# A hybrid gMLP and retention encoder on one core: retention scores of the first 128 keys from float32r halves, one tile later

## The chip, the core and the metric

The kernel runs on one core of a Trainium2 chip. The metric is device time in microseconds (us) for one execution. Times of whole executions are medians of several runs; everything about single instructions comes from one profiled execution.

Names of engines in the profile: PE is the matrix engine, PEld its weight loads, DVE the vector engine, ACT the scalar engine, POOL the engine that here mostly issues transfers, SP the queue that streams the weights in.

## The reference, cut to what matters

A two-layer encoder step on 256 prompt frames and 32 sample frames (288 columns in all). Layer 0 mixes tokens with a gated MLP, layer 1 with retention; each is followed by a SwiGLU network. All in float32. The change lies in the retention block of layer 1, which has 8 heads:

```python
def retention_block(q, k, v, s0, decay, inner, zeta, blk_decay):
    scores = jnp.einsum('bhqd,bhkd->bhqk', q, k) * decay[None]
    intra = jnp.einsum('bhqk,bhkv->bhqv', scores, v)
    cross = jnp.einsum('bhqd,bhdv->bhqv', q, s0) * inner[None, :, :, None]
    s_new = blk_decay[None, :, None, None] * s0 + jnp.einsum(
        'bhkd,bhkv->bhdv', k * zeta[None, :, :, None], v)
    return intra + cross, s_new
```

A head has 256 dimensions for q and k (rotated by `rope` first) and 512 for v. The output of a head is normalised, gated by `silu(g)` and multiplied by `w_out`.

## The kernel before, in words

**Weights.** All weights lie in one stream in the order of use, cut into chunks of 8 blocks of 128x128. SP loads a chunk as float32 (`raw`). ACT makes its high half `whi` in float32r, the reduced form that PE takes in one pass (`split`, L454), and DVE the low half `wlo`, the rest (L455). There are four buffers of each half; `prep(c + 3)` stands where PE begins chunk c, so a chunk is made while three others lie ahead of it.

**The main products.** Activations are held as halves too, transposed (features on partitions, 288 columns). One block is three matmuls of 288 columns: high by high (L106), low by high (L107), high by low (L108). A tile is one output tile of 128 features: 16 blocks, 48 matmuls, two chunks. `core.tick()` runs after each tile, and `core.after(n, f)` puts off a piece of work by n tiles. PE executes in the order in which the program is written. DVE, ACT and POOL have an order of their own, which a scheduler made from the dependencies and from costs it assumes; each of them works through its list strictly in that order.

**Retention.** `b_in` gives a head 4 tiles of v, 2 of k, 2 of q and 4 of g. Heads 0 and 1 take g, v, k, q in this order; the others v, k, q, and g of heads 2 and 3 comes behind q of head 3, of 6 and 7 behind q of head 7. Heads 2, 3 and 7 follow the q of the head before without g between. What happens around the change:

- `turn` (at once after the second k or q tile, two tiles later for head 0) rotates k or q on DVE with `rope` (L668 to L673) into `rk` or `rq`. For k, ACT repeats the 32 sample columns twice (L717), so that the sample has 96 stationary columns; then DVE transposes k (L740) and POOL sends it through memory to turn it to rows (`k_room`, `kw`). For q, DVE and ACT make `qi`.
- `k_split` scales and splits the rows of k into `kh`, `kl`, `ks`.
- `scores` (`core.after(self.wait, ...)` behind q; `self.wait` is 3 for head 0 and 2 for the others) has six matmuls in float32: two of 128 keys by 256 prompt queries (L770), two of the second 128 keys by the second 128 queries (L772), two of 96 stationary columns by 32 sample queries (L774). Each float32 matmul shows up as two in the profile. DVE multiplies by the decay `dec` into `pf` and `psf` (L779 to L781); ACT and DVE split these into `ph`, `pl` and `r_ps` (L454, L455, L783, L784).
- `attend` stands one tile behind the last of `scores`, `k_split` and `v_split`: 28 float32r matmuls (`os`, `ss`, `ob`, `sp`), the first of which reads `r_ps`. The head's output is then normalised and moved through memory (`o_room`, `of`); `o_gate` multiplies it by the gate (L894) and splits it for `b_out`.
- v goes from DVE transposes (`tv`, L700) through memory (`v_room`, `vw`, `vz`, on POOL) to `v_split` three tiles later (ACT and DVE write `vv`).

Small buffers of the rotation and of the scores (`rt1`, `rt2`, `qf`, `pf`, `psf`) each have a place in the pool of the retention stage. `PostNorm.tmp` gives out six rotating buffers of another pool, used by the normalisations before and behind.

Of the kernel before, what the change touches and what calls it, by code (L numbers as in the profile page):

```python
# [10 lines left out]
F32 = mybir.dt.float32  # L11
F32R = mybir.dt.float32r
I32 = mybir.dt.int32
AF = mybir.ActivationFunctionType
ALU = mybir.AluOpType
# [4 lines left out]
P = 128  # L20
D = 2048
KT = D // P
NP = 256
NS = 32
NT = NP + NS
# [3 lines left out]
NR = 3 * NS  # L29
# [146 lines left out]
def fourth(nc):  # L176

    def mm(out, w, x, **kw):
        nc.tensor.matmul(turned(out, 4), w, turned(x, 4), **kw)

    return mm
# [271 lines left out]
def split(nc, hi, lo, f):  # L453
    nc.scalar.copy(hi, f)  # L454
    nc.vector.tensor_tensor(lo, f, hi.bitcast(F32), ALU.subtract)  # L455
# [176 lines left out]
def retention(core, cst, x, y, lnp, prev, ins, st_p_out, st_s_out):  # L632
    tc, nc = core.tc, core.nc
    xh, xl = x
    xs = lambda k: (xh[:, k, :NT], xl[:, k, :NT])
    mm, mm4 = nc.tensor.matmul, fourth(nc)
    with ExitStack() as es:
        pool = es.enter_context(tc.tile_pool(name="ret", bufs=1, reuse_waits="tile"))
# [10 lines left out]
        nc.gpsimd.dma_start(inn, ins["inner"])  # L649
        ln = PostNorm(core, cst, x, y, lnp, 2)  # L650
        pss = pool.tile([P, 2 * NS], F32R, tag="pss", name="r_ps")
        zero = pool.tile([P, NS], F32, name="r_zero")
        nc.gpsimd.memset(zero, 0.0)
        nc.scalar.copy(pss[:NR, NS:], zero[:NR, :])
        heads = {}
# [7 lines left out]
            return t[:, :4 * NT].rearrange("p (b i s) -> p b i s", b=9, i=4)  # L663

        def rope(dst, a, b, cos, sin, nm):
            t1 = pool.tile([P, NT], F32, tag="rt1", name=f"rt1{nm}", bufs=1)
            t2 = pool.tile([P, NT], F32, tag="rt2", name=f"rt2{nm}", bufs=1)
            nc.vector.tensor_tensor(t1, a[:, :NT], cos, ALU.mult)  # L668
            nc.vector.tensor_tensor(t2, b[:, :NT], sin, ALU.mult)
            nc.vector.tensor_tensor(dst[:, 0, :NT], t1, t2, ALU.subtract)  # L670
            nc.vector.tensor_tensor(t1, a[:, :NT], sin, ALU.mult)
            nc.vector.tensor_tensor(t2, b[:, :NT], cos, ALU.mult)
            nc.vector.tensor_tensor(dst[:, 1, :NT], t1, t2, ALU.add)  # L673

        class Head:
            def __init__(self, h):
                self.h = h
                self.wait = 3 if h == 0 else 2
                self.ps = {}
                self.left = {"k", "v", "s"}  # L680
                self.open = {"o", "g"}
                self.dec = pool.tile([P, NT], F32, tag="dec", name=f"dec{h}")
                nc.gpsimd.dma_start(self.dec, ins["decay"][h])
                self.sg = pool.tile([P, 4, NT], F32, tag="rsg", name=f"rsg{h}", bufs=2)

            def evac(self, m, ps):
                h = self.h
                if m < 32:
                    self.ps[m % 2] = ps
                    if m % 2:  # L690
                        turn = lambda p=dict(self.ps): self.turn(m, p)
                        if h == 0:
                            core.after(2, turn)
                        else:
                            turn()
                elif m < 64:
                    i = m % 4
                    if i == 0:
                        self.tv = blocks(f"tv{h}", h)
                    nc.vector.transpose(self.tv[:, :, i, :], ps[:, :NT])  # L700
                    if i == 3:
                        self.v_move()
                else:
                    i = m % 4
                    nc.scalar.activation(self.sg[:, i, :], ps[:, :NT], AF.Silu)
                    if i == 3:
                        core.after(1, lambda: self.o_gate("g"))

            def turn(self, m, ps):
                h = self.h  # L710
                isk = m >= 16
                nm = ("k" if isk else "q") + str(h)
                r = pool.tile([P, 2, NP + (NR if isk else NS)], F32, tag="kr" if isk else "qr", name="r" + nm)
                rope(r, ps[0], ps[1], cs[:, 0, :], cs[:, 1, :], nm)
                if isk:
                    self.kr = r
                    nc.scalar.copy(r[:, :, NT:].rearrange("p d (r n) -> p d r n", r=2),  # L717
                                   r[:, :, NP:NT].unsqueeze(2).broadcast_to([P, 2, 2, NS]))
                    self.k_move()
                else:  # L720
                    self.qr = r
                    qf = pool.tile([P, 2, NS], F32, tag="qf", name=f"qf{h}")
                    qi = pool.tile([P, 160], F32R, tag="qi", name=f"qi{h}")
                    self.qi = qi[:, 20:20 + 4 * NS].rearrange("p (d a n) -> p d a n", d=2, a=2)
                    nc.vector.tensor_tensor(qf, r[:, :, NP:], inn[:, h, :].unsqueeze(1).broadcast_to([P, 2, NS]), ALU.mult)
                    split(nc, self.qi[:, :, 0, :], self.qi[:, :, 1, :], qf)
                    core.after(self.wait, self.scores)

            def proceed(self, what, i=3):
# [35 lines left out]
            def scores(self):  # L765
                h = self.h
                self.proceed("s")
                b = core.bank(f"sc{h}")
                for d in range(2):
                    mm(b[:, 0:NP], self.kr[:, d, 0:P], self.qr[:, d, 0:NP], start=d == 0, stop=d == 1)  # L770
                for d in range(2):
                    mm(b[:, NP:NP + P], self.kr[:, d, P:NP], self.qr[:, d, P:NP], start=d == 0, stop=d == 1)  # L772
                for d in range(2):
                    mm(b[:NR, 384:384 + NS], self.kr[:, d, NP:], self.qr[:, d, NP:], start=d == 0, stop=d == 1)  # L774
                pf = pool.tile([P, 384], F32, tag="pf", name=f"pf{h}")
                self.ph = pool.tile([P, 384], F32R, tag="ph", name=f"ph{h}")
                self.pl = pool.tile([P, 384], F32R, tag="pl", name=f"pl{h}")
                psf = pool.tile([P, NS], F32, tag="psf", name=f"psf{h}")
                nc.vector.tensor_tensor(pf[:, :NP], b[:, :NP], self.dec[:, :NP], ALU.mult)  # L779
                nc.vector.tensor_tensor(pf[:, NP:], b[:, NP:384], self.dec[:, :P], ALU.mult)  # L780
                nc.vector.tensor_tensor(psf[:NR, :], b[:NR, 384:384 + NS], self.dec[:NR, NP:], ALU.mult)  # L781
                r = slice(2 * NS, NR)
                nc.scalar.copy(pss[:NR, :NS], psf[:NR, :])  # L783
                nc.vector.tensor_tensor(pss[r, :NS], psf[r, :], pss[r, :NS].bitcast(F32), ALU.subtract)  # L784
                split(nc, self.ph, self.pl, pf)

            def v_move(self):
                h = self.h
# [135 lines left out]
        for grp in range(2):  # L924
            a, b, c, d = order[4 * grp:4 * grp + 4]
# [12 lines left out]
def hybrid_step(ctx, tc, ins, outs):  # L938
# [34 lines left out]
    ln = gmlp(core, cst, x, y, lnp, ins, outs["v"], lambda s: load(s + 4))  # L973
    ln = ffn(core, cst, x, y, lnp, 0, ln)
    ln = retention(core, cst, x, y, lnp, ln, ins, outs["st_p"], outs["st_s"])
    ffn(core, cst, x, y, lnp, 1, ln, outs["yT"])
    core.flush()
# [86 lines left out]
```

## Time and profile before

| | |
|---|---|
| median of 3 runs | 2777.39 us (2776.27 to 2778.74) |
| the profiled execution | 2780.03 us, its span 2778.3 us |
| PE busy | 2767.8 us |
| DVE, ACT, POOL busy | 1664.5, 1241.0, 140.9 us |
| PE's weight loads busy | 2753.8 us |
| scores, attend of head 2 on PE | from 1330.86 us, from 1338.63 us |

The span goes from the first to the last instruction; the execution has 1.7 us more around it. Matmul records overlap, since the matmuls are pipelined, so what a matmul costs is read from the distance between the starts of neighbours, or from the chain of waits, where each piece is given the time up to the next. Times of single instructions are counted from the start of the span.

### The profile page before, as it was taken

The numbers are of one execution on the slowest core, as the hardware profiler recorded it, in microseconds if no ns is written. First come the engines' busy times: TensorE is split into PE (matmuls) and PEld (weight loads), VectorE is DVE, ScalarE is ACT, GpSimd is POOL, SyncE is SP. The second block draws the span as 40 slices with busy tenths as digits, with TensorE's granted clock in tenths as the row PEclk, the third lists the DMA queues.
The fourth block names the chain that finished last, engine by engine and source line by source line (L and its number), as shares of the span: only waits on it lengthen the run. The fifth ranks groups of instructions, "written<-read, shape, count | busy, mean of one in ns | idle before, by whom it ended". The sixth has DMA issues, their size and how long they took to land.

```text
span 2778.3 us, 51413 instructions
## 1 busy us (share of the span) xinstructions
PE 2767.8 (100%) x21590; PEld 2753.8 (99%) x21590; DVE 1664.5 (60%) x2360; ACT 1241.0 (45%) x1644; POOL 140.9 (5%) x241
## 2 busy tenths in 40 slices
PE   9999999999999999999999999999999999999998
PEld 9999999999999999999999999999999999999998
DVE  5688854444444466767765666767844455444465
ACT  5455643433333344644443444445634333343343
POOL 1100000000000000012200111200000000000001
PEclk9999999999999999999999999999999999999999
DMA  8655555555555555567765676765555555555553
GB/s 277 214 186 167 168 175 175 175 174 172 172 174 174 176 175 176 190 209 232 232 196 175 195 221 214 229 197 171 173 173 172 173 174 175 175 174 173 172 173 125
DMA packets 147529, 515.51 MB, mean 186 GB/s; under 512 B 18064, under 2 KB 22176, under 8 KB 147264
## 3 DMA queue, kind: packets, MB, share of 16 engines
q1 hardware_dynamic: 132928, 473.33, 52.0%
q0 software_dynamic: 14224, 38.59, 4.7%
q8 instruction: 169, 2.77, 0.4%
q14 instruction: 64, 0.52, 0.0%
q10 hardware_dynamic: 144, 0.29, 0.0%
HBM read 486.98 MB, written 25.17 MB: 184 GB/s over the span
## 4 chain that ended last, share of the span: by engine, by line
PE 97%; DMA 1%; DVE 1%; ACT 0%; issue 0%; POOL 0%; SPq 0%; DVEq 0%; POOLq 0%; ACTq 0%
PE af_in L107 13%; PE af_in L108 13%; PE af_in L106 13%; PE ab_in L106 7%; PE ab_in L107 7%; PE ab_in L108 7%; PE af_out L106 6%; PE af_out L107 6%; PE af_out L108 6%; PE ab_out L107 2%; PE ab_out L106 2%; PE ab_out L108 2%; PE aa_in L108 2%; PE aa_in L106 2%; PE aa_in L107 2%; PE aa_out L107 1%
## 5 line engine op out<-in xcount | busy, mean ns | idle before, releaser
L455 DVE TENSOR_TENSOR wlo<-raw,whi 128x1024 fp32r<-128x1024 f32 (+1 forms) x892 | 1086.2, 1219 | 885.5 <-ACT whi L454 881.4
L454 ACT CAST whi<-raw 128x1024 fp32r<-128x1024 f32 (+1 forms) x892 | 933.1, 1047 | 1384.5 <-issue 336.5
L107 PE MATMUL af_in<-xl,whi 128*128 128x288 f32 (+1 forms) x2816 | 812.6, 289 | 0.0
L106 PE MATMUL af_in<-xh,whi 128*128 128x288 f32 (+1 forms) x2816 | 812.3, 288 | 0.0
L108 PE MATMUL af_in<-xh,wlo 128*128 128x288 f32 (+1 forms) x2816 | 812.3, 288 | 0.0
L108 PEld LDWEIGHTS af_in<-xh,wlo 128*128 128x128 f32 x2816 | 527.7, 187 | 0.0
L107 PEld LDWEIGHTS af_in<-xl,whi 128*128 128x128 f32 x2816 | 527.7, 187 | 0.0
L106 PEld LDWEIGHTS af_in<-xh,whi 128*128 128x128 f32 x2816 | 527.7, 187 | 0.0
L106 PE MATMUL ab_in<-xh,whi 128*128 128x288 f32 (+1 forms) x1536 | 443.9, 289 | 0.0
L107 PE MATMUL ab_in<-xl,whi 128*128 128x288 f32 (+1 forms) x1536 | 443.3, 289 | 0.0
L108 PE MATMUL ab_in<-xh,wlo 128*128 128x288 f32 (+1 forms) x1536 | 443.2, 289 | 0.0
L108 PE MATMUL af_out<-hh,wlo 128*128 128x288 f32 x1408 | 405.9, 288 | 0.0
L106 PE MATMUL af_out<-hh,whi 128*128 128x288 f32 x1408 | 405.9, 288 | 0.0
L107 PE MATMUL af_out<-hl,whi 128*128 128x288 f32 x1408 | 405.9, 288 | 0.0
L107 PEld LDWEIGHTS ab_in<-xl,whi 128*128 128x128 f32 x1536 | 287.9, 187 | 0.3
L106 PEld LDWEIGHTS ab_in<-xh,whi 128*128 128x128 f32 x1536 | 287.9, 187 | 0.3
L108 PEld LDWEIGHTS ab_in<-xh,wlo 128*128 128x128 f32 x1536 | 287.9, 187 | 0.0
L107 PEld LDWEIGHTS af_out<-hl,whi 128*128 128x128 f32 x1408 | 263.8, 187 | 0.0
L106 PEld LDWEIGHTS af_out<-hh,whi 128*128 128x128 f32 x1408 | 263.8, 187 | 0.0
L108 PEld LDWEIGHTS af_out<-hh,wlo 128*128 128x128 f32 x1408 | 263.8, 187 | 0.0
L108 PE MATMUL aa_in<-xh,wlo 128*128 128x288 f32 x512 | 148.1, 289 | 1.2 <-DVE wlo L455 1.1
L106 PE MATMUL aa_in<-xh,whi 128*128 128x288 f32 x512 | 148.7, 290 | 0.0
(240 smaller groups left out, 2873.9 us busy)
## 6 DMA issues: line engine op xcount, KB each, us to landing
raw<-in_wpack_dram SPq DMA_DIRECT2D x887, 512.0 KB, 3.3
v_room<-tv POOLq DMA_DIRECT2D x32, 144.0 KB, 5.1
of<-o_room POOLq DMA_DIRECT2D x32, 144.0 KB, 5.2
vw<-v_room POOLq DMA_DIRECT2D x8, 512.0 KB, 5.2
out_st_s_dram<-sso POOLq DMA_DIRECT2D x16, 256.0 KB, 2.6
out_st_p_dram<-so POOLq DMA_DIRECT2D x16, 256.0 KB, 2.8
o_room<-to POOLq DMA_DIRECT2D x8, 512.0 KB, 3.8
y<-in_xT_dram SPq DMA_DIRECT2D x8, 288.0 KB, 5.2
```

The lines of the kernel that those rows point to most:

```text
L106: mm(ps, hi, xh, start=first, stop=False)
L107: mm(ps, hi, xl, start=False, stop=False)
L108: mm(ps, lo, xh, start=False, stop=last)
L454: nc.scalar.copy(hi, f)
L455: nc.vector.tensor_tensor(lo, f, hi.bitcast(F32), ALU.subtract)
```

## The change

For the first 128 keys, `rq` and `rk` are split into float32r halves (`q0a`, `q0b`, `k0a`, `k0b` for head 0, and so on), by one copy on ACT and one subtraction on DVE each. `scores` then takes three float32r products for each of the two halves of the head's dimensions, six matmuls of 256 columns, in the place of the two float32 ones. The other scores stay in float32. The sample's product keeps 96 stationary columns, but takes the last 96 columns of k as they are (64 prompt keys and the 32 sample keys), so the copy that repeated the sample's columns goes; only the last 32 rows of the result are used, and three copies of 32 rows on ACT take the place of one of 96. The split of `pf` is done in two pieces. `self.wait` is 3 for all heads. The small buffers come from `prev.tmp`, the six rotating ones.

```diff
-        zero = pool.tile([P, NS], F32, name="r_zero")
+        zero = prev.tmp("r_zero")[:, :NS]
...
-            t1 = pool.tile([P, NT], F32, tag="rt1", name=f"rt1{nm}", bufs=1)
-            t2 = pool.tile([P, NT], F32, tag="rt2", name=f"rt2{nm}", bufs=1)
+            t1 = prev.tmp(f"rt1{nm}")
+            t2 = prev.tmp(f"rt2{nm}")
...
-                self.wait = 3 if h == 0 else 2
+                self.wait = 3
...
-                r = pool.tile([P, 2, NP + (NR if isk else NS)], F32, tag="kr" if isk else "qr", name="r" + nm)
+                r = pool.tile([P, 2, NT], F32, tag="kr" if isk else "qr", name="r" + nm)
+                parts = [pool.tile([P, 2, P if isk else NP], F32R, tag=nm[0] + x, name=nm + x) for x in "ab"]
                 rope(r, ps[0], ps[1], cs[:, 0, :], cs[:, 1, :], nm)
                 if isk:
                     self.kr = r
-                    nc.scalar.copy(r[:, :, NT:].rearrange("p d (r n) -> p d r n", r=2),
-                                   r[:, :, NP:NT].unsqueeze(2).broadcast_to([P, 2, 2, NS]))
                     self.k_move()
+                    self.kp = parts
+                    split(nc, *parts, r[:, :, :P])
...
+                    self.qp = parts
+                    split(nc, *parts, r[:, :, :NP])
                     core.after(self.wait, self.scores)
...
-                for d in range(2):
-                    mm(b[:, 0:NP], self.kr[:, d, 0:P], self.qr[:, d, 0:NP], start=d == 0, stop=d == 1)
+                (kh, kl), (qh, ql) = self.kp, self.qp
+                prods = [(l[:, d, :], r[:, d, :]) for d in range(2) for l, r in ((kh, qh), (kh, ql), (kl, qh))]
+                for i, (l, r) in enumerate(prods):
+                    mm4(b[:, 0:NP], l, r, start=i == 0, stop=i == len(prods) - 1)
...
-                    mm(b[:NR, 384:384 + NS], self.kr[:, d, NP:], self.qr[:, d, NP:], start=d == 0, stop=d == 1)
-                pf = pool.tile([P, 384], F32, tag="pf", name=f"pf{h}")
+                    mm(b[:NR, 384:384 + NS], self.kr[:, d, NT - NR:], self.qr[:, d, NP:], start=d == 0, stop=d == 1)
+                pf = [prev.tmp(f"pf{h}{i}") for i in range(2)]
...
-                nc.vector.tensor_tensor(psf[:NR, :], b[:NR, 384:384 + NS], self.dec[:NR, NP:], ALU.mult)
                 r = slice(2 * NS, NR)
-                nc.scalar.copy(pss[:NR, :NS], psf[:NR, :])
+                nc.vector.tensor_tensor(psf[r, :], b[r, 384:384 + NS], self.dec[r, NP:], ALU.mult)
+                for i in range(3):
+                    nc.scalar.copy(pss[i * NS:(i + 1) * NS, :NS], psf[r, :])
                 nc.vector.tensor_tensor(pss[r, :NS], psf[r, :], pss[r, :NS].bitcast(F32), ALU.subtract)
-                split(nc, self.ph, self.pl, pf)
+                split(nc, self.ph[:, :NP], self.pl[:, :NP], pf[0][:, :NP])
+                split(nc, self.ph[:, NP:], self.pl[:, NP:], pf[1][:, :P])
```

How the instructions stand, first on PE at the scores of head 1. Before, they come right behind tile `ab_in_192`, the first v tile of head 2; `rq` and `rk` are the rotated q and k:

```order
L108 MATMUL ab_in_192_14178<-xh,wlo_14106 128x3x24x4
L770 MATMUL sc_14244<-rq_14164,rk_14002 128x256 x2
L772 MATMUL sc_14244<-rq_14164,rk_14002 128x128 x2
L774 MATMUL sc_14244<-rq_14164,rk_14002 96x32 x2
L106 MATMUL ab_in_193_14262<-xh,whi_14135 128x3x24x4
```

The same place after, behind tile `ab_in_193`; `q1a` and `k1a` are the high halves, `q1b` and `k1b` the low ones:

```order
L108 MATMUL ab_in_193_14267<-xh,wlo_14204 128x3x24x4
L179 MATMUL sc_14329<-q1a,k1a 128x4x16x4
L179 MATMUL sc_14329<-q1b,k1a 128x4x16x4
L179 MATMUL sc_14329<-q1a,k1b 128x4x16x4
L179 MATMUL sc_14329<-q1a,k1a 128x4x16x4
L179 MATMUL sc_14329<-q1b,k1a 128x4x16x4
L179 MATMUL sc_14329<-q1a,k1b 128x4x16x4
L777 MATMUL sc_14329<-rq_14170,rk_14018 128x128 x2
L779 MATMUL sc_14329<-rq_14170,rk_14018 96x32 x2
L106 MATMUL ab_in_194_14356<-xh,whi_14233 128x3x24x4
```

The scores stand 48 matmuls later, and `attend` with them, for heads 1 to 7; for head 0 they stand where they stood.

On POOL, from the output of head 1 to v and k of head 2, before (`o_room` and `of` are the output's way, `v_room` and `vw` that of v, `k_room` and `kw` that of k):

```order
L882 DMA o_room_14413<-tz_14409 32x512
L883 DMA o_room_14413<-to_14408 128x2x512
L886 DMA of_14410<-o_room_14413 32x9x128 x4
L463 DMA v_room_14546<-tv_14242 32x9x128 x4
L464 DMA vw_14544<-v_room_14546 128x2x512
L465 DMA vz_14545<-v_room_14546 32x512
L463 DMA k_room_14700<-tk_14696 32x9x64 x4
```

And after:

```order
L889 DMA o_room_14507<-tz_14503 32x512
L463 DMA v_room_14578<-tv_14265 32x9x128
L890 DMA o_room_14507<-to_14502 128x2x512
L463 DMA v_room_14578<-tv_14265 32x9x128 x2
L893 DMA of_14504<-o_room_14507 32x9x128 x4
L463 DMA v_room_14578<-tv_14265 32x9x128
L463 DMA k_room_14722<-tk_14718 32x9x64
L464 DMA vw_14576<-v_room_14578 128x2x512
L465 DMA vz_14577<-v_room_14578 32x512
L463 DMA k_room_14722<-tk_14718 32x9x64 x3
```

The two moves are now interleaved: `vw` stands behind the first issue of `k_room`, which waits for the transposed k of head 2. The same holds where head 3 follows 2 and head 7 follows 6.

On ACT, the stretch of head 2 from the casts of v to the split of the scores, before (`whi` rows are casts of weight chunks):

```order
L717 COPY rk_14686<-rk_14686 128x2x64
L454 CAST vv_14707<-vw_14544 128x1024
L454 CAST vv_14707<-vz_14545 32x512
L804 CAST vv_14707<-vz_14545 32x512
L454 CAST whi_14789<-raw_14788 128x1024
L454 CAST whi_14819<-raw_14818 128x1024
L454 CAST whi_14864<-raw_14863 128x1024
L454 CAST whi_14894<-raw_14893 128x1024
L754 ACTIVATE kh_14774<-kw_14699,r_zt 128x256 x2
L760 ACTIVATE ks_14776<-kw_14699,r_zt 32x256 x2
L454 CAST qi_14858<-qf_14857 128x2x32
L454 CAST whi_14948<-raw_14947 128x1024
```

And after:

```order
L454 CAST whi_14811<-raw_14810 128x1024
L454 CAST whi_14841<-raw_14840 128x1024
L454 CAST vv_14742<-vw_14576 128x1024
L454 CAST vv_14742<-vz_14577 32x512
L811 CAST vv_14742<-vz_14577 32x512
L454 CAST whi_14903<-raw_14902 128x1024
L454 CAST whi_14933<-raw_14932 128x1024
L454 CAST q2a<-rq_14870 128x512
L454 CAST qi_14882<-qf_1_14881 128x2x32
L757 ACTIVATE kh_14888<-kw_14721,r_zt 128x256 x2
L763 ACTIVATE ks_14890<-kw_14721,r_zt 32x256 x2
L454 CAST whi_14969<-raw_14968 128x1024
```

The casts of v have moved behind two more weight casts (two weight casts stand between them and `q2a`, where four stood before `kh`), and the cast `q2a` is new.

More of the change, by code (lines that the diff above doesn't have):

```diff
@@ L716, in turn @@
                     self.kr = r
-                    nc.scalar.copy(r[:, :, NT:].rearrange("p d (r n) -> p d r n", r=2),
-                                   r[:, :, NP:NT].unsqueeze(2).broadcast_to([P, 2, 2, NS]))
                     self.k_move()
+                    self.kp = parts
+                    split(nc, *parts, r[:, :, :P])
                 else:
                     self.qr = r
-                    qf = pool.tile([P, 2, NS], F32, tag="qf", name=f"qf{h}")
+                    qf = prev.tmp(f"qf{h}")[:, :2 * NS].rearrange("p (d n) -> p d n", d=2)
                     qi = pool.tile([P, 160], F32R, tag="qi", name=f"qi{h}")
@@ L773, in scores @@
                 for d in range(2):
-                    mm(b[:NR, 384:384 + NS], self.kr[:, d, NP:], self.qr[:, d, NP:], start=d == 0, stop=d == 1)
-                pf = pool.tile([P, 384], F32, tag="pf", name=f"pf{h}")
+                    mm(b[:NR, 384:384 + NS], self.kr[:, d, NT - NR:], self.qr[:, d, NP:], start=d == 0, stop=d == 1)
+                pf = [prev.tmp(f"pf{h}{i}") for i in range(2)]
                 self.ph = pool.tile([P, 384], F32R, tag="ph", name=f"ph{h}")
                 self.pl = pool.tile([P, 384], F32R, tag="pl", name=f"pl{h}")
-                psf = pool.tile([P, NS], F32, tag="psf", name=f"psf{h}")
-                nc.vector.tensor_tensor(pf[:, :NP], b[:, :NP], self.dec[:, :NP], ALU.mult)
-                nc.vector.tensor_tensor(pf[:, NP:], b[:, NP:384], self.dec[:, :P], ALU.mult)
-                nc.vector.tensor_tensor(psf[:NR, :], b[:NR, 384:384 + NS], self.dec[:NR, NP:], ALU.mult)
+                psf = prev.tmp(f"psf{h}")[:, :NS]
+                nc.vector.tensor_tensor(pf[0][:, :NP], b[:, :NP], self.dec[:, :NP], ALU.mult)
+                nc.vector.tensor_tensor(pf[1][:, :P], b[:, NP:384], self.dec[:, :P], ALU.mult)
                 r = slice(2 * NS, NR)
-                nc.scalar.copy(pss[:NR, :NS], psf[:NR, :])
+                nc.vector.tensor_tensor(psf[r, :], b[r, 384:384 + NS], self.dec[r, NP:], ALU.mult)
+                for i in range(3):
+                    nc.scalar.copy(pss[i * NS:(i + 1) * NS, :NS], psf[r, :])
                 nc.vector.tensor_tensor(pss[r, :NS], psf[r, :], pss[r, :NS].bitcast(F32), ALU.subtract)
-                split(nc, self.ph, self.pl, pf)
+                split(nc, self.ph[:, :NP], self.pl[:, :NP], pf[0][:, :NP])
+                split(nc, self.ph[:, NP:], self.pl[:, NP:], pf[1][:, :P])
             def v_move(self):
```

## The prediction

> **What bounds the kernel now.** I read the page first, for its busy times, then the waits of PE (in total, times, the longest).
>
> ```profile
> PE 2767.8 (100%) x21590; PEld 2753.8 (99%) x21590; DVE 1664.5 (60%) x2360; ACT 1241.0 (45%) x1644; POOL 140.9 (5%) x241
> ```
>
> ```profile
> PE aa_in L108 <- DVE wlo L455: 1.1, 3, 0.5
> PE warm L959 <- POOL g_nrm L503: 1.0, 1, 1.0
> ```
>
> PE is busy for 2767.8 of the span's 2778.3 us, and in the whole run it waited four times for other engines, 2.1 us together, all in the first stage (`aa_in`, `warm`). In the retention stage it waits for nobody. So two things can move the time: the number and price of matmuls, and a new wait of PE. A change that only gives DVE, ACT or POOL more to do costs nothing until it makes PE wait.
>
> Next I read the chain of waits at head 2, where each row's time runs up to the start of the next, and one window of a stage that has only 288-column matmuls (window, length, busy time and count of PE, PEld, DVE, ACT and POOL, then PE's granted clock, 1.00).
>
> ```profile
> 1330.86 0.86 PE sc L770 x4
> 1331.73 0.44 PE sc L772 x4
> 1332.17 0.28 PE sc L774 x4
> 1332.45 0.21 PE ab_in L106
> ...
> 1338.63 1.12 PE os L179 x5
> ...
> 1340.20 1.99 PE ob L179 x9
> ```
>
> ```profile
> 600.00:900.00 300.00, 300.00 (x2370) 300.00 (x2369) 147.30 (x161) 112.55 (x130) 0.00 (x0) 1.00 0.53 174
> ```
>
> The two float32 matmuls that are replaced (four records, L770) take 0.86 us of PE per head. A float32r matmul takes 300/2370 = 0.127 us at 288 columns and 1.99/9 = 0.221 us at 512.
>
> **The matmuls.** Six float32r matmuls of 256 columns come in. No row shows that width. The line through the two widths rises by (0.221 - 0.127)/224 = 0.00042 us a column, so 256 columns give 0.127 - 32 x 0.00042 = 0.113 us, and six 0.68. Saved: 0.86 - 0.68 = 0.18 us a head, **1.44 us for eight heads**. Bounds from the nearest rows: no dearer than a 288-column one (six at 0.127 are 0.76: 0.10 a head, 0.8 in all), no cheaper than half a 512-column one (six at 0.1105 are 0.66: 0.20 a head, 1.6 in all). I take 1.44, since 288 columns are the near row. L772 and L774 keep their shapes, 0.44 and 0.28, and the dear first float32r matmul behind them (0.21 where 0.127 is usual) stays. The change of form at the entrance cost nothing before and moves from L770 to L772.
>
> The Trainium skill ("FP8 and Floating Point Precision", on number formats) says that true float32 takes four passes through the array. Four passes against three would save a quarter of 0.86, 0.215 a head and 1.7 us in all; the rows give a little less, since each matmul costs something beyond its columns (0.127 x 512/288 is 0.226, not 0.221). Both round to the same forecast.
>
> **The new splits.** ACT gains two copies a head (128x512 for q, 128x256 for k), the split of `ph` in two and two more copies of 32 rows, and loses the repeat of the sample's columns. DVE gains two subtractions and a split in two. Rows of head 2 on ACT and DVE (start, duration, instruction, then idle time before and what ended it):
>
> ```profile
> 1306.45 1.05 ACT L454 CAST whi<-raw 128x1024 fp32r<-128x1024 f32 x1 [1.99 <-PE ab_in L107]
> ...
> 1317.03 0.30 ACT L717 COPY rk<-rk 128x128 f32<-128x128 f32 x1 [0.36 <-DVE rk L673]
> 1317.24 1.04 ACT L454 CAST vv<-vw 128x1024 fp32r<-128x1024 f32 x1
> ...
> 1334.04 0.51 ACT L454 CAST ph<-pf 128x384 fp32r<-128x384 f32 x1 [2.05 <-DVE pf L780]
> 1334.46 0.21 ACT L783 CAST r_ps<-psf 96x32 fp32r<-96x32 f32 x1
> ```
>
> ```profile
> 1307.54 1.23 DVE L455 TENSOR_TENSOR wlo<-raw,whi 128x1024 fp32r<-128x1024 f32 x1 [0.50 <-ACT whi L454]
> ...
> 1319.11 1.22 DVE L455 TENSOR_TENSOR vv<-vw,vv 128x1024 fp32r<-128x1024 f32 x1
> 1320.36 0.68 DVE L455 TENSOR_TENSOR vv<-vz,vv 32x512 fp32r<-32x512 f32 x1
> ...
> 1327.82 0.46 DVE L673 TENSOR_TENSOR rq<-rt1q,rt2q 128x288 f32<-128x288 f32 x1
> ...
> 1333.39 0.41 DVE L779 TENSOR_TENSOR pf<-sc,dec 128x256 f32<-128x256 f32 x1
> ...
> 1334.58 0.56 DVE L455 TENSOR_TENSOR pl<-pf,ph 128x384 fp32r<-128x384 f32 x1 [0.49 <-ACT ph L454]
> 1335.17 0.18 DVE L784 TENSOR_TENSOR r_ps<-psf,r_ps 32x32 fp32r<-32x32 f32 x1
> ```
>
> Between 384 columns (0.51 on ACT, 0.56 on DVE) and 1024 (1.05, 1.23) the slope is 0.54/640 and 0.67/640. That gives 0.62 and 0.40 us on ACT for 512 and 256 columns, 0.70 and 0.43 on DVE. A split of 384 in two pays the fixed part once more: 0.51 - 384 x 0.54/640 = 0.19 on ACT, 0.16 on DVE. Two more copies at 0.21 are 0.42. ACT: 0.62 + 0.40 + 0.19 + 0.42 - 0.30 = 1.3 us a head more; DVE: 0.70 + 0.43 + 0.16 = 1.3.
>
> What hides it is the ring of weight buffers. The cast of 1306.45 was released by PE's last reading of its buffer, when three chunks lay ready. A chunk is 24 matmuls, 24 x 0.127 = 3.05 us, so the new one is wanted 9.1 us after the release. Its low half ends at 1308.77, 2.3 us after the cast began: 6.8 us to spare. An engine may thus come up to 6.8 us late with one chunk before PE sees it, and 1.3 us a head is far below that; the idle 1.99 before the cast also takes up a delay. Cost on the path: nothing. If that cover were gone, it would be at most 8 x 1.3 x 2 = 21 us.
>
> **One tile later.** A tile is 48 x 0.127 = 6.1 us. For head 2 `scores` moves from 1330.86 to about 1337.0 and `attend` from 1338.63 to 1344.7. Two waits of PE could be new.
>
> First, `scores` now needs `q2b`. The rotation ends at 1328.28 (L673). In its new place the subtraction of v lies ahead of it on DVE (1.22 + 0.68), then come the cast (0.62), at most one low half of weights (1.23), `qi` and the subtraction itself (0.2 + 0.70): 1332.9, so 4 us before PE asks. With the old wait of two tiles, PE would have asked at 1330.86 and waited 2 us. So the later place is what makes the halves free.
>
> Second, the first matmul of `attend` reads `r_ps`, whose last writer ended at 1335.35, 3.3 us ahead of 1338.63. This distance loses 0.19 (ACT's second half of `ph`), 0.42 (two copies) and at most 0.16 (DVE): 2.5 us are left.
>
> **POOL's queue.** Issues are in order there, and one that waits holds all behind it.
>
> ```profile
> 1311.82 0.75 POOL L464 DMA_DIRECT2D vw<-v_room  x1 [5.95 <-DMA v_room<-tv]
> ...
> 1317.81 2.43 POOL L463 DMA_DIRECT2D k_room<-tk  x4 [4.71 <-DVE tk L740]
> ```
>
> ```profile
> ACT vv L454 <- DMA vw<-v_room: 6.1, 5, 1.4
> ```
>
> ```profile
> DMA to landing us min/median/max: 4.6/5.2/6.0
> ```
>
> For heads 2, 3 and 7 `vw` now stands behind the first `k_room`, which was issued at 1317.81 when k was transposed. So `vw` goes out at about 1317.81 + 2.43/4 = 1318.4 instead of 1311.82 and lands 5.2 us later (the last row, of tile `vw`), at 1323.6. ACT's cast of v, at 1317.24 before, stands two weight casts (6.1 us) later: 1323.3. A wait of some 0.3 us, within the 1.4 that ACT already waited there at worst without PE noticing. Behind the cast on ACT stand the weight casts, with their 6.8 us. `dec` of the next head waits for the scores and comes a tile later; it is next read eight tiles on. Cost: nothing.
>
> **The end of a group.** For heads 3 and 7 `attend` moves towards `b_out`. Head 3:
>
> ```profile
> 1414.90 2.46 POOL L886 DMA_DIRECT2D of<-o_room  x4 [4.46 <-issue]
> ```
>
> ```profile
> 1440.03 1.35 DVE L894 TENSOR_TENSOR rsg<-of,rsg 128x1152 f32<-128x1152 f32 x1
> ```
>
> The gated product at 1440.03 starts with the last g tile; `of` is issued by 1417.4, a tile later by 1423.5, and even with 6 us to land it is there by 1430. Nothing.
>
> The buffers from `prev.tmp` (eight for each head, six in rotation) are each reused when their reader is a head or half a head past: no wait. **Sum: -1.44 us.** The profiled execution, 2780.03 us, is 2.6 above the median; the saving is the same from either: 2778.6 for such an execution, **2776.0 for the median** (2777.39 - 1.44).
>
> **The rivals.**
>
> *The loads set the pace.* Every matmul brings its own load of 128 weight columns. Two loads that follow each other in `b_in`:
>
> ```profile
> 1213.45 0.19 PEld L106 LDWEIGHTS ab_in<-xh,whi 128*128 128x128 f32 x1
> ...
> 1213.58 0.19 PEld L107 LDWEIGHTS ab_in<-xl,whi 128*128 128x128 f32 x1
> ```
>
> If a load's 0.19 us no longer hid under a narrower matmul, six would take 6 x 0.19 = 1.14 us, 0.28 a head more than now: +2.2 us, 2779.6. Against it: loads start every 0.13 us here, so they overlap each other and the matmuls, and the float32 records of 128 columns (0.44/4 = 0.11, L772) have a load each as well. The Trainium skill ("TensorE: Matmul & The Clock Gate", on measured speedups of packing) says that loads overlap matmuls in flight only when they address other rows of the array; by that rule the six would cost more than the four. The trace disagrees: full 128-row loads of 0.19 us start 0.13 us apart, and so do the matmuls (0.127). Chance 0.05, with every outcome in which nothing is saved.
>
> *`attend` waits for `r_ps`, and the kernel gets slower.* The 2.5 us left hold if DVE and ACT take the scores as promptly as before. Both are in-order, and a weight chunk ahead of the chain costs 1.05 + 1.23 = 2.3 us. Two such chunks (4.6) overrun 2.5 by 2.1 us; seven moved heads lose 7 x 2.1 = 14.7: 2776.0 + 14.7 = 2790.7. It decides (over 0.2%) from about 1 us a head, a chain 3.5 us later than worked out. For it: a weight chunk is due every 3.05 us. Against: one low half already ends at the chain's start today, and the distance was 3.3 still. Chance 0.05.
>
> *v comes late.* If `vw` lost another round trip on POOL (5.95 of waiting and 5.2 to land, 11.2 in all), ACT would wait 11.5 us and PE 11.5 - 6.8 = 4.7 at heads 2, 3 and 7: 14.1 us, 2790.1. For it: three waits of two chains now interleave in one queue. Against: the wait must be eight times the longest of today. Chance 0.03.
>
> **How the numbers follow.** This kernel's measurement can tell about 0.2%, 5.6 us, from no change; my saving is a quarter of that. The forecast has 0.85, the loads 0.05, both "within". The two slower cases have 0.08, and 0.02 stays for a gain that no row shows. So faster 0.02, same 0.90, slower 0.08. The range: lowest run less the largest saving, 2776.27 - 1.6 = 2774.7, to 2779.5, the first rival's time, which also covers the highest run with no saving; the slower cases are left out.
>
> **What would show it.** Right: in the chain of waits `sc` of the first 128 keys takes 0.65 to 0.70 us for six, PE still waits for nobody from 1160 to 1860 us, and ACT's wait for `vw` stays near a microsecond. Wrong: six matmuls at 0.86 or more, a row "PE os" or "PE sc" among the waits, or PE waiting for `wlo` behind heads 2, 3 and 7.

## The result, and the profile after

The changed kernel takes 2804.2 us (median of five runs, 2802.28 to 2808.18), the kernel before on the same chip 2776.27 (2775.99 to 2778.74). The ratio is 1.0099, 95% interval 1.0088 to 1.0110: 28 us slower, where 1.4 us faster was forecast.

The engine row of the page and the waits of PE, after:

```profile
PE 2792.3 (100%) x21606; PEld 2779.8 (99%) x21606; DVE 1673.0 (60%) x2384; ACT 1249.3 (45%) x1676; POOL 141.2 (5%) x241
```

```profile
PE warm L966 <- POOL g_nrm L503: 1.0, 1, 1.0
```

PE waits no more than before, less in fact; no row names `sc`, `os` or `wlo`. It is busy 24.5 us longer, with 16 matmuls more. So the time has gone into matmuls that cost more, not into a wait. The scores are not the place where it went. The chain of waits at head 2 after the change (start, time up to the next piece, what), which answers to the rows shown of before:

```profile
1336.54 0.68 PE sc L179 x6
1337.22 0.44 PE sc L777 x4
1337.67 0.28 PE sc L779 x4
1337.95 0.21 PE ab_in L106
...
1344.13 1.12 PE os L179 x5
1345.25 0.48 PE ss L179 x2
1345.73 2.00 PE ob L179 x9
1347.73 2.67 PE sp L179 x12
1350.40 0.13 PE ab_in L106
```

Six matmuls in 0.68 us, as forecast. The later place shows too: `scores` at 1336.54, `attend` at 1344.13. Inside `attend` small amounts are new: `ss` 0.48, where head 1 of the kernel before has 0.45 (its row stands further down).

The lost time shows in windows that hold nothing but 288-column matmuls of `b_in` (window, its length, busy time and number of matmuls that reach into it, granted clock, DMA share, GB/s). Before, behind `attend` of head 0 and of head 1:

```profile
1235.00:1265.00 30.00, 30.00 (x239) 1.00 0.83 244
1295.00:1325.00 30.00, 30.00 (x240) 1.00 0.82 264
```

After, the same two windows:

```profile
1235.00:1265.00 30.00, 30.00 (x239) 1.00 0.77 241
1295.00:1325.00 30.00, 30.00 (x227) 1.00 0.83 255
```

Behind head 0 nothing has changed. Behind head 1, PE does 227 matmuls in 30 us instead of 240, busy all the time, at a granted clock of 1.00 in both. From the single records: the starts are 126.7 ns apart in the one case and 133.3 in the other, for all three products of a block and all weight buffers alike. I call these the two rhythms. After the change the long one holds from each of the last seven `attend` until the next `scores` (or the matmul `cen` at 1912.3): 4025 distances, times 6.67 ns, make **26.8 us**. These seven `attend` themselves add 0.06 us each (6.268 for 6.208 us), 0.4 together; the scores take 1.4 off. The sum is +25.8 us. It can be held against the stage itself, from its first `b_in` matmul to `cen`, first before and then after:

```profile
1112.82 0.29 PE L106 MATMUL ab_in<-xh,whi 128*128 128x290 f32 x1
1888.90 0.29 PE L277 MATMUL cen<-cen,one_r 128*128 128x288 f32 x1
```

```profile
1110.44 0.29 PE L106 MATMUL ab_in<-xh,whi 128*128 128x290 f32 x1
1912.30 0.30 PE L277 MATMUL cen<-cen,one_r 128*128 128x288 f32 x1
```

That is 776.08 us before and 801.86 after, 25.8 more: the sum accounts for all of it. The spans of the two profiled executions differ by less (2800.0 - 2778.3 = 21.7) because the one of before came to this stage 2.4 us later and took 1.6 us longer behind it. The rows of single products say the same, before and then after:

```profile
L106 PE MATMUL ab_in<-xh,whi 128*128 128x288 f32 (+1 forms) x1536 | 443.9, 289 | 0.0
L106 PE MATMUL ab_out<-r_oh,whi 128*128 128x288 f32 x512 | 147.6, 288 | 0.0
```

```profile
L106 PE MATMUL ab_in<-xh,whi 128*128 128x288 f32 (+1 forms) x1536 | 451.8, 294 | 0.0
L106 PE MATMUL ab_out<-r_oh,whi 128*128 128x288 f32 x512 | 150.3, 293 | 0.0
```

### The profile page after: what moved, and what is told of

Read it like the earlier page. It is cut to its first block, busy times and chain, and to the rows that moved or that the text cites. A ratio compares the mean times of both kernels' runs of the same rounds, so it can differ in the third digit from the quotient of the medians.

```text
span 2800.0 us, 51502 instructions
## 1 busy us (share of the span) xinstructions
PE 2792.3 (100%) x21606; PEld 2779.8 (99%) x21606; DVE 1673.0 (60%) x2384; ACT 1249.3 (45%) x1676; POOL 141.2 (5%) x241
## 4 chain that ended last, share of the span: by engine, by line
PE 100%; DVE 0%; DVEq 0%; POOL 0%; issue 0%; POOLq 0%
PE af_in L107 13%; PE af_in L106 13%; PE af_in L108 13%; PE ab_in L106 7%; PE ab_in L107 7%; PE ab_in L108 7%; PE af_out L106 6%; PE af_out L108 6%; PE af_out L107 6%; PE ab_out L106 2%; PE ab_out L107 2%; PE ab_out L108 2%; PE aa_in L107 2%; PE aa_in L106 2%; PE aa_in L108 2%; PE aa_out L106 1%
## 5 line engine op out<-in xcount | busy, mean ns | idle before, releaser
L106 PE MATMUL ab_in<-xh,whi 128*128 128x288 f32 (+1 forms) x1536 | 451.8, 294 | 0.0
L107 PE MATMUL ab_in<-xl,whi 128*128 128x288 f32 (+1 forms) x1536 | 451.2, 294 | 0.0
L108 PE MATMUL ab_in<-xh,wlo 128*128 128x288 f32 (+1 forms) x1536 | 451.2, 294 | 0.0
L106 PE MATMUL ab_out<-r_oh,whi 128*128 128x288 f32 x512 | 150.3, 293 | 0.0
L108 PE MATMUL ab_out<-r_oh,wlo 128*128 128x288 f32 x512 | 150.3, 293 | 0.0
```

The lines of the kernel that those rows point to most:

```text
L106: mm(ps, hi, xh, start=first, stop=False)
L107: mm(ps, hi, xl, start=False, stop=False)
L108: mm(ps, lo, xh, start=False, stop=last)
```

## The experiments

**First, which part does it: the place of `attend` and `scores` in the order, the six products, or the buffers?**

The changed kernel with the old wait:

```diff
-                self.wait = 3
+                self.wait = 3 if h == 0 else 2
```

> The changed kernel with the old wait of two tiles for heads 1 to 7, so scores and attend stand where they stood before; the halves, the buffers and the sample's columns stay changed. In the changed kernel the 288-column matmuls start 0.133 us apart from head 1's attend on, where 0.127 is usual. Theory of the place (the later place of attend brings PE into the slow rhythm): 0.127 everywhere, and PE waits up to 2 us a head for the low half of q, so 2775 to 2790 us. Theory of the six products (the new float32r scores bring it about) and theory of the addresses (the moved buffers do): still 0.133, 2800 us or more.

It took 2815.84 us, a ratio of 1.0133 (1.0103 to 1.0162). The long rhythm is still there, behind six of the eight heads (228 matmuls in the window from 1295), so the later place is not needed for it. What the later place was for shows in the waits of PE, 10.1 us in all for the halves of q, which is most of what this run lies above the changed kernel:

```profile
PE sc L179 <- DVE q5b L455: 1.7, 1, 1.7
PE sc L179 <- DVE q1b L455: 1.7, 1, 1.7
...
PE sc L179 <- DVE q2b L455: 0.9, 1, 0.9
```

The other way round, the kernel before with a wait of three tiles for all heads and nothing else:

```diff
-                self.wait = 3 if h == 0 else 2
+                self.wait = 3
```

> The kernel before with the wait of three tiles for all heads, and nothing else changed. Theory of the place: the slow rhythm of 0.133 us appears, 2800 to 2808 us. Theories of the six products and of the addresses: 0.127 as before, 2776 to 2779 us.

2776.6 us, ratio 0.9997 (0.9986 to 1.0008), 239 matmuls in the window. The later place costs nothing.

The changed kernel with its scores in float32, the halves made and not used:

```diff
-                for i, (l, r) in enumerate(prods):
-                    mm4(b[:, 0:NP], l, r, start=i == 0, stop=i == len(prods) - 1)
+                for d in range(2):
+                    mm(b[:, 0:NP], self.kr[:, d, 0:P], self.qr[:, d, 0:NP], start=d == 0, stop=d == 1)
```

> The changed kernel with the two float32 matmuls back in the place of the six float32r ones; the halves are still made, and not read. Theory of the six products: 0.127 us everywhere, 2777 us. Theories of the place and of the addresses: 0.133 from head 1 on, 2803 us or more.

2804.81 us, 1.0093 (1.0064 to 1.0120), 227 in the window: the six products are not needed for the long rhythm.

The kernel before with only the small buffers taken from the six rotating ones:

```diff
-        zero = pool.tile([P, NS], F32, name="r_zero")
+        zero = prev.tmp("r_zero")[:, :NS]
...
-            t1 = pool.tile([P, NT], F32, tag="rt1", name=f"rt1{nm}", bufs=1)
-            t2 = pool.tile([P, NT], F32, tag="rt2", name=f"rt2{nm}", bufs=1)
+            t1 = prev.tmp(f"rt1{nm}")
+            t2 = prev.tmp(f"rt2{nm}")
...
-                    qf = pool.tile([P, 2, NS], F32, tag="qf", name=f"qf{h}")
+                    qf = prev.tmp(f"qf{h}")[:, :2 * NS].rearrange("p (d n) -> p d n", d=2)
...
-                psf = pool.tile([P, NS], F32, tag="psf", name=f"psf{h}")
+                psf = prev.tmp(f"psf{h}")[:, :NS]
```

> The kernel before with the small buffers (zero, rt1, rt2, qf, psf) taken from the six rotating ones, so that the buffers behind them in the pool move; the rest as before. Theory of the addresses: the slow rhythm appears, 2800 us or more. Theories of the place and of the six products: 0.127, 2776 to 2779 us.

2804.33 us, 1.0091 (1.0062 to 1.0120), with 228. PE's matmuls are those of before, one for one, and no wait is new. What differs is where buffers lie: what is allocated behind `r_zero` moves down, `rk` by 128 bytes, `rq` by 2432. Among the moved buffers PE reads only these two. The run also shares buffers, so by itself it can't tell the sharing from the move.

**Second, is it the sharing or the place, and the place of what?** The kernel before with one buffer that nobody uses, of 128 bytes a partition:

```diff
         zero = pool.tile([P, NS], F32, name="r_zero")
+        pool.tile([P, 32], F32, name="r_pad")
```

> The kernel before with one unused buffer of 128 bytes a partition ahead of `dec`: all that is allocated behind it, `rk` and `rq` among it, stands 128 bytes higher; no instruction is changed, none added. Theory of the place: the 288-column matmuls fall to 133.3 ns after most `attend`, 2802 to 2806 us. Theory of the shared buffers or of the six products: 126.7 ns, 2776 to 2779 us.

2805.66 us, 1.0099 (1.0070 to 1.0129). Not one instruction has changed. Its windows behind heads 0 and 1, and its chain at `attend` of head 1, then the same chain of the kernel before:

```profile
1235.00:1265.00 30.00, 30.00 (x239) 1.00 0.82 250
1295.00:1325.00 30.00, 30.00 (x228) 1.00 0.78 247
```

```profile
1280.49 1.12 PE os L179 x5
1281.61 0.48 PE ss L179 x2
1282.09 2.00 PE ob L179 x9
1284.09 2.67 PE sp L179 x12
```

```profile
1282.08 1.12 PE os L179 x5
1283.20 0.45 PE ss L179 x2
1283.65 1.99 PE ob L179 x9
1285.64 2.65 PE sp L179 x12
```

The same with 256 bytes (`[P, 64]` for `[P, 32]`):

> The kernel before with one unused buffer of 256 bytes a partition at the same spot: everything behind it stands 256 bytes higher. Theory of the place, with 256 bytes as its step: 126.7 ns, 2776 to 2779 us, as if nothing had moved. If the place counts otherwise (any move of the buffers, or a longer step), 133.3 ns and 2802 to 2806 us. Theory of the shared buffers: 126.7 ns.

2777.02 us, 0.9997 (0.9986 to 1.0009), 239 in the window. So moving as such is harmless; as far as moves of 128 and 256 bytes can tell, what counts is the place within a step of 256 bytes. Before the change `rk` starts 64 bytes past a multiple of 256, with the 128 bytes 192 past one; no run tried another place. The unused 128 bytes behind `rk`, then directly ahead of it:

```diff
+                if isk and h == 0:
+                    pool.tile([P, 32], F32, name="r_pad")
```

> The kernel before with the unused 128 bytes a partition behind `rk`: `rk`, `dec`, `rsg`, `vz` stay, and `rq` and what follows it stand 128 bytes higher. Theory of the place: if the place of `rq` (the operand that moves past the weights) decides, 133.3 ns and 2802 to 2806 us; if that of `rk` (the stationary one) decides, 126.7 ns and 2776 to 2779 us. Theory of the shared buffers: 126.7 ns.

> The kernel before with the unused 128 bytes a partition directly ahead of `rk`: `dec`, `rsg` and `vz` stay, `rk` and what follows it stand 128 bytes higher (that what follows costs nothing by itself, the run with the bytes behind `rk` showed: 126.7 ns). Theory of the place, narrowed to `rk`, the stationary operand of `scores`: 133.3 ns after seven of eight `attend`, 2802 to 2807 us. If one of `dec`, `rsg` or `vz` did it: 126.7 ns, 2776 to 2779 us.

Behind `rk`: 2777.62 us, 1.0005 (0.9994 to 1.0017). Ahead of it: 2804.81, 1.0101 (1.0072 to 1.0130). The windows from 1295, in this order:

```profile
1295.00:1325.00 30.00, 30.00 (x239) 1.00 0.83 260
```

```profile
1295.00:1325.00 30.00, 30.00 (x228) 1.00 0.80 248
```

The two differ in the place of `rk` alone. It is the stationary operand of the float32 scores, the one that PE's weight loads bring in; where the moving one, `rq`, lies made no difference here.

The changed kernel with `rk` put back (two small buffers take their room earlier, which moves what follows by 128 bytes):

```diff
+        pool.tile([P, 3, 6], F32, tag="gst", name="r_gst")
+        pool.tile([P, 3, 2], F32, tag="gmv", name="r_gmv")
         nc.gpsimd.memset(zero, 0.0)
```

> The changed kernel; two small buffers of the group norm (128 bytes a partition together) take their room earlier, so that the rotated keys `rk` stand at the byte at which they stood before the change (204864) and the rotated queries `rq` 768 bytes under theirs (214592 for 215360), where the changed kernel has them 128 and 896 bytes lower. Nothing else moves in the order of work. Theory of the place (where `rk` and `rq` stand, counted in steps of 256 bytes, sets the phase in which TensorE enters and leaves `scores`, and with it the rhythm after `attend`): the 288-column matmuls start 126.7 ns apart after every `attend`, and the time is 2774.5 to 2776.5 us. Theory of the shared buffers (the step results in the six turning buffers do it, wherever the rest stands): 133.3 ns after seven of the eight `attend`, 2802 to 2806 us. Theory of the six products: as the second.

2806.3 us, 1.0102 (1.0072 to 1.0131): the expectation failed. Now even head 0 is followed by the long rhythm. The same edit on the changed kernel with float32 scores:

> The changed kernel with its scores of the first 128 keys in plain float32, as before, and `rk` at its byte of before (204864); buffers shared, wait 3, 96 columns, splits made and not used. Theory of the place: 126.7 ns, 2776 to 2779 us, where the same kernel with `rk` 128 bytes lower took 2804.8. If sharing the buffers or the shorter `rk` also counts: 133.3 ns, 2802 to 2807 us.

2776.88 us, 1.0000 (0.9988 to 1.0011), 239. So with float32 scores the loss goes by the place of `rk` in all ten kernels that have them (the swap below among them): 192 in the four with the long rhythm, 64 in the six without. Why head 0 escapes in those four is open. With six products a second stationary operand comes in, the halves `k0a`, `k0b` and so on, and they have a place of their own. I moved the halves alone into the other half of the step, with `rk` put back and without:

```diff
+        for tag in ("ka", "kb"):
+            pool.tile([P, 2, P], F32R, tag=tag, name=f"r_{tag}")
         nc.gpsimd.memset(zero, 0.0)
```

> The changed kernel with `rk` in the half of a 256-byte step that it had before (byte 206912, 64 past a multiple of 256) and the float32r halves of the keys in the other half (192448, 192 past one). The changed kernel itself has 192 and 192, the run with both at 64 was slow as well. If the stationary operands of `scores` set the phase, this place gives one of the two rhythms, and the theory doesn't say which: 126.7 ns and 2774.5 to 2776.5 us, or 133.3 ns and 2802 to 2807 us. Theory that the six products turn the rhythm wherever they stand: 133.3 ns.

> The changed kernel with `rk` as the change leaves it (192 past a multiple of 256) and the float32r halves of the keys at 64 past one (192320). As the run above: 126.7 ns and 2774.5 to 2776.5 us, or 133.3 ns and 2802 to 2807 us, by the theory of the place; 133.3 ns by the theory that the six products turn the rhythm wherever they stand. If both of these places are slow, no place of the keys alone mends the changed kernel.

| `rk`, past 256 bytes | halves of k | us | ratio | rhythm behind `attend` |
|---|---|---|---|---|
| 192 | 192 (as changed) | 2804.2 | 1.0099 (1.0088 to 1.0110) | 133.3, seven heads |
| 64 | 64 | 2806.3 | 1.0102 (1.0072 to 1.0131) | 133.3, eight heads |
| 192 | 64 | 2805.96 | 1.0105 (1.0076 to 1.0134) | 133.3, eight heads |
| 64 | 192 | 2775.6 | 0.9997 (0.9985 to 1.0008) | 126.7 throughout |

One place of the four keeps the short rhythm, with all of the change in. In the last two rows the halves also lie some 14,700 bytes lower than in the second; that it is the half of the step that counts for them, as it does for `rk`, is taken over from `rk` and not shown by itself.

**Third, do the places hold the rhythm up, or only set it?** First the kernel of the table's last row again, for its time:

> The changed kernel with `rk` at 64 and the float32r halves of the keys at 192 past a multiple of 256, as in the run that kept 126.7 ns after every `attend`, timed in more rounds. The prediction's sum for the change (1.4 us less in eight `scores`, nothing else on the path) then has to show against the kernel before: 2775.5 to 2776.3 us where that takes 2777.2, a ratio of 0.9993 to 0.9997. If the cheaper scores are given back somewhere even in the fast rhythm: a ratio of 0.9999 to 1.0002.

2776.99 us beside 2777.29, ratio 0.9998 (0.9989 to 1.0007): it falls between the two expectations, and the interval holds both the forecast saving and none. The stage itself tells more (see below).

The changed kernel with its buffers left where the change puts them, and one of the 28 matmuls of `attend`, the last, in another form (it reads its 512 columns in plain order):

```diff
-                        mm4(sp[d], l, r, start=i == 0, stop=i == len(prods) - 1)
+                        f = mm if d == 1 and i == len(prods) - 1 else mm4
+                        f(sp[d], l, r, start=i == 0, stop=i == len(prods) - 1)
```

> The changed kernel, places as the change leaves them; the last of the twelve products of `states` reads its 512 columns in their plain order and not turned (eight of 13,000 matmuls). Theory of the place: the slow rhythm is set by what TensorE does around `attend`, and one matmul of another form between `attend` and the weights that follow can end it, as the plain 288-column matmul of `cen` does in the trace after: 126.7 ns and 2774.5 to 2776.5 us if it does. If the rhythm outlives it, as it outlives the scores of some heads: 133.3 ns and 2802 to 2806 us. Theory that buffers kept slow by their place slow the weights' matmuls all the while: 133.3 ns.

2775.88 us, 0.9996 (0.9986 to 1.0006). Its windows and its chain at `attend` of head 1:

```profile
1235.00:1265.00 30.00, 30.00 (x239) 1.00 0.78 240
1295.00:1325.00 30.00, 30.00 (x239) 1.00 0.86 268
```

```profile
1286.81 1.12 PE os L179 x5
1287.93 0.45 PE ss L179 x2
1288.38 1.99 PE ob L179 x9
1290.37 2.42 PE sp L179 x11
1292.79 0.23 PE sp L917
```

Here the long rhythm never begins: `ss` takes 0.45 already, ahead of the plain matmul of this head. So the matmul did not end the long rhythm, as I had put it; the one behind head 0 sent PE on differently, and it met `attend` of head 1, and every later one, as the kernel before does. The places didn't move and the loss is gone. They set the rhythm, they don't hold it up.

The kernel before with the room of `r_ps` and `qi` swapped:

```diff
-("pss", 2 * NS), ("qi", 160))
+("qi", 160), ("pss", 2 * NS))
```

> The kernel before with two buffers swapped: `r_ps`, the stationary operand of the first matmul of `attend`, stands 640 bytes higher (its place in a 256-byte step moves by 128), the buffer of `qi` 256 bytes lower (its place stays); `rk` stays. If the place of any stationary operand that TensorE loads on the way in can turn the rhythm: 133.3 ns after `attend`, 2802 to 2807 us. If only the operands of `scores` do it, since the phase comes from there: 126.7 ns, 2776 to 2779 us.

2778.29 us, 1.0002 (0.9992 to 1.0012). Behind `attend` the starts stay 126.7 ns apart, but `attend` itself now takes 6.264 us as in the long rhythm. The rhythm and the time are those of the second expectation; the dearer `attend` neither had: the place of `r_ps` acts, within `attend` only.

## Why the prediction was wrong

**What held.** The six matmuls: 0.68 us forecast, 0.68 measured, and L777, L779 and the dear first matmul behind them keep 0.44, 0.28 and 0.21. The wait for `q2b`: its last writer ends 6.4 us before `scores` (4 were worked out), and at the old place PE did wait, 0.9 to 1.7 us for `qb` alone at each of seven heads (2 were worked out). `r_ps`: ready 3.5 us ahead of `attend`, 2.5 forecast; no wait. `vw`: ACT waited for it 5 times, 1.4 us at the longest, the same as before. In head 2 of the changed kernel the two writers and the wait are these rows:

```profile
1329.44 0.68 DVE L455 TENSOR_TENSOR q2b<-rq,q2a 128x512 fp32r<-128x512 f32 x1
```

```profile
1340.49 0.18 DVE L790 TENSOR_TENSOR r_ps<-psf,r_ps 32x32 fp32r<-32x32 f32 x1 [0.27 <-ACT r_ps L789]
```

```profile
ACT vv L454 <- DMA vw<-v_room: 5.5, 5, 1.4
```

None of the rivals came about: no load set the pace of the six, and PE waited for neither `r_ps` nor v. All the signs of being right were there, and none of those of being wrong, while the time was 1% off: they looked at the scores and at waits, and not at the price of the matmuls around them.

**What failed** is the step "The buffers from `prev.tmp` ... no wait", and with it the sum. I asked of these buffers only when they come free. That their leaving moves all that is allocated behind them, and that a moved operand could change the price of matmuls that the change doesn't touch, had no term, no rival and no chance. In the changed kernel it is `rk` that moved, by the 128 bytes that `r_zero` left. Nor did I ask where the new halves would lie: with `rk` back at its place the loss stayed (2806.3 us), and went only when the halves lay elsewhere too (2775.6). The sum took 0.127 us for each 288-column matmul of the stage as given. The missing term is 4025 x 6.67 ns = 26.8 us, nearly twenty times the term that I worked out.

**Whether the 1.44 us are there** once the rhythm is kept. Whole executions can't show it. The three runs with all of the change and the short rhythm (2775.6, 2776.99, 2775.88) lie below the kernel before in each case, and the means of all their executions (27, against 42 of before on the same chips) differ by -1.0 us, give or take 0.6. But no single ratio interval excludes 1, and the run with nothing but the later place, which has the very matmuls of the kernel before, lies 1.5 us under it in its mean.

The stage shows it, from its first `b_in` matmul to `cen`. It took 776.08 us in the kernel before and in each of four others that have float32 scores and the short rhythm (the later place, 256 bytes, 128 bytes behind `rk`, float32 scores with `rk` put back). With `rk` at 64 and the halves at 192 it took 774.60 in both profiled executions; the second of them:

```profile
1115.01 0.29 PE L106 MATMUL ab_in<-xh,whi 128*128 128x290 f32 x1
1889.61 0.29 PE L277 MATMUL cen<-cen,one_r 128*128 128x288 f32 x1
```

So the saving is there, 1.48 us, where 1.44 was forecast; with the one plain matmul it is 1.17 (774.91). Both ways of mending, the places and the one plain matmul, also beat the changed kernel by 27 to 29 us.

**What stays open.** In the records the two cases can be told apart as PE enters `attend`. The distance from the last `b_in` matmul to `os`, and what follows, worked out from the starts in ns, at head 1:

```
kernel                               last to os   next seven distances            behind
before                                   128      236 230 219 220 220 219 226     126.7
before, unused 128 bytes                 131      232 230 218 219 225 235 239     133.3
changed                                  132      231 229 219 220 223 236 238     133.3
changed, rk 64 and halves 192            128      236 230 219 220 220 219 226     126.7
changed, one plain matmul                127      237 230 218 220 220 219 226     126.7
```

Over 16 runs and eight heads (all but the swap of `r_ps`), 71 entries had 126 to 128 ns and 57 had 131 or 132; behind every one of the 71 the short rhythm holds, behind every one of the 57 the long one. The run with the old wait has one head of each kind at the same places: head 4 enters with 127 and is followed by 126.7, its neighbours with 131, and are followed by 133.3. So 4 ns at one point go with the one or the other of two steady rhythms.

The choice is made earlier than that, though. In the tile between `scores` and `attend` the matmuls start 122 to 123 ns and about 125 ns behind the starts of their weight loads, in turn. The last of these 48 has 122 or 123 in all 71 short entries, and 124 to 126 in all 57 long ones. Which of the two comes first is settled within the first 13 matmuls behind `scores` in 127 of the 128 entries; the other is head 1 of the run with the old wait, at its 19th, behind a stretch at half the clock. That fits an influence of the operands of `scores`; what stands in `attend` comes too late for its own head.

What in the chip keeps the two rhythms apart, and why 128 bytes under a stationary operand turn this order round, no run here shows; I could read the rule, but not predict from the places which of the four would be the good one.

## What to carry to other kernels

When a change takes small buffers away, or adds some, list which operands of PE move, even if no instruction does; then compare the distance of neighbouring starts in a stretch that the change doesn't touch before looking for a wait. A busy PE at full granted clock can still run 5% slower there, and no view of waits shows it. Before judging such a change, run it with its stationary operands at several places, moved by unused room; to put the old one back was not enough here. Of four places three cost 1% and would have condemned a change that by itself saves 1.5 us. And read so small a saving from a stage in which the bottleneck never waits: here it repeated to 0.01 us in five profiles, where whole executions differ by 2 us and more.

## What the runs showed that I had not expected

- Float32r matmuls of 288 columns have two steady distances, 126.7 and 133.3 ns, at the same granted clock of 1.00; those of 512 columns in `attend` go by 220 ns each in the one, and by 219, 222 and 226 in turn in the other.
- An unused buffer of 128 bytes costs 28 us of 2777; one of 256 bytes nothing.
- In the run with the old wait, PE's 1.7 us of waiting at head 1 was followed by a stretch of 3.4 us (from 1276.3 to 1279.7) in which the granted clock was 0.50 and the matmuls started 240 ns apart. A wait of the same 1.7 us at head 5 was followed by none, so the wait alone doesn't decide it. A window inside that stretch:

```profile
1276.80:1278.50 1.70, 1.70 (x9) 0.50 0.68 200
```
